# A decoder layer with GpSimd's long element-wise operations divided into pieces

## The chip, the cores and the metric

The program runs on one NeuronCore of a Trainium2 chip. Its time is the device time of one execution in microseconds (us), and a kernel's figure is the median of its runs. A core has five engines that the text names as the profile does: PE (TensorE, with PEld for its weight loads), DVE (VectorE), ACT (ScalarE), POOL (GpSimd) and SP (SyncE, which here only starts DMAs). SBUF is the on-chip memory that all engines read, PSUM the one that PE writes its products to. "Words" below are 32-bit words per partition: an operation of 128x1024 has 1024 words on each of 128 partitions.

## What is computed

One inference step of one decoder layer, for a prompt of 1024 tokens and for 8 sequences with 4 new tokens each, 1056 tokens in all with a model width of 1024. All is float32.

```python
def decoder_layer(x, cond, pos, conv_prev, s0, mla_attend, lp):
    ...
    x = x + 0.5 * mods[:, 2] * swiglu_ffn(h, lp['ffn1_wi'], lp['ffn1_wo'])
    h = rms_norm(x, lp['norm_mix']) * (1 + mods[:, 4]) + mods[:, 3]
    qkv, z, b_raw, a_raw, q_raw, ckv_raw, kr_raw = split_cols(h @ lp['w_in'], IN_SPLITS)
    gdn_out, new_conv, new_s = gdn_mixer(qkv, z, b_raw, a_raw, conv_prev, s0, ...)
    qn, qr, c, kr = mla_project(q_raw, ckv_raw, kr_raw, pos, ...)
    ctx = mla_attend(qn, qr, c, kr, lp['mla_w_uk'], lp['mla_kn_norm'])
    mla_out = jnp.einsum('bthr,rhv->bthv', ctx, lp['mla_w_uv']).reshape(B, T, MLA_HEADS * MLA_V)
    mix = jnp.concatenate([gdn_out, mla_out.astype(gdn_out.dtype)], axis=-1) @ lp['w_out']
    x = x + mods[:, 5] * mix
    ...
    x = x + 0.5 * mods[:, 8] * swiglu_ffn(h, lp['ffn2_wi'], lp['ffn2_wo'])
```

`gdn_mixer` is a gated delta rule: a short causal convolution over q, k and v, then a recurrence over a state of 64x64 words for each head, `S_t = a_t (I - b_t k_t k_t^T) S_{t-1} + b_t k_t v_t^T`, `o_t = S_t^T q_t`. The prompt's recurrence is done in chunks of 64 tokens with a triangular inverse for each chunk; the 8 short sequences take the four steps one by one. `mla_attend` is attention over latent keys, for the short sequences over 4096 cached positions that are read through a page table.

## The kernel before

The program has one stage after the other: feed-forward 1 (to about 840 us), the projections and what is done at once with their results (840 to 1290 us, `mixer_in`), the attention of the prompt (1290 to 1700 us), the recurrences (1700 to 2037 us), the output projection with feed-forward 2 behind it. Beside the prompt's attention and the recurrences, the attention of the short sequences over the cache (`sample_gen`) runs as a filler.

Each matrix product is made of three PE passes (`mm3`, L120 to L122): operands are split into a rounded high part (ACT makes `hi`, e.g. `whi`) and a remainder (`lo`, e.g. `wlo`, a subtraction on POOL or DVE).

**Projections.** `proj_weights` loads 128 columns of `w_in`, ACT casts `whi` (L645), POOL subtracts `wlo` (L646, 1024 words); three such slices are prepared ahead. PE multiplies them with the four token blocks into `pp`. What follows a slice runs as generators that are advanced between the blocks: the convolution's taps on DVE (`cy`, L885, 1080 words, three for each slice), the norms (a chain of ten small DVE operations, `rsqrt`, L697 to L701), the scaling by decay factors on POOL (`scaled`, L916, 512 words), the decay matrices (`decay`, L852), and the keys' gains (`kcat`, L1211). `mla_q_finish` takes the attention queries tile by tile, nine tiles one after the other: a DMA brings the rows `mq`, ACT squares, DVE sums and scales (L1133, L1138), POOL multiplies by the gains (L1139, 768 words), DVE and POOL rotate (`rope`: DVE L1078, L1080, L1082 and L1083, POOL L1079 and L1081), a DMA takes them away. `invert` makes the triangular inverses: POOL scales `M` (L1044), DVE runs 31 steps of two operations (`inv` L1054, `M` L1056), POOL masks the results `X` (L1060, L1064).

**Recurrences.** The prompt's recurrence `scan_gen` puts many small products on PE, with DVE operations such as `S` (L1456) between them. `gdn_sample` does the four steps of the short sequences on POOL alone: the state `gS` and its scratch `gt` have 2048 words, and each step has five operations of 2048 words and two summing trees (1024, 512, 256, 128, 64 and 32 words), all through the helper `mul` at L1515. POOL also issues the gathers of the cache (`ck`, `krh`, L628). The filler `sample_gen` needs, for each 32 keys per partition, the chain `rsqrt` on tiles `rsk` and `pv` of 128 words (DVE L699 to L701), whose end ACT copies to `rx` (L1826) for PE's `psr` (L1836).

**Order.** On POOL the operations of the three middle stages run in the order in which the program text issues them (`manual_schedule`). On the other engines and queues a planner with estimated times sets the order; each engine then works through its list in order, waiting on semaphores.

Of the kernel before, what the change touches and what calls it, by code (L numbers as in the profile page):

```python
# [12 lines left out]
ALU = mybir.AluOpType  # L13
# [4 lines left out]
P = 128  # L18
# [13 lines left out]
H = 8  # L32
# [38 lines left out]
def f(ap):  # L71
    return ap.bitcast(F32)
# [12 lines left out]
class Kernel:  # L85
# [7 lines left out]
    def pool(self, name, **kw):  # L93
        return self.ctx.enter_context(self.tc.tile_pool(reuse_waits="tile", name=name, **kw))


# [535 lines left out]
    def proj_weights(self, eng=None):  # L632

        nc = self.nc
        w = self.i["w_in"][0]
        pieces = self.worder.pop(0)
        m = sum(n for _, n in pieces)
        raw = self.wraw.tile([P, KT, P], F32, tag="wraw", name="wraw")
# [4 lines left out]
        hi = self.wsp.tile([P, KT, P], F32R, tag="w", name="whi", bufs=self.wbufs)  # L643
        lo = self.wsp.tile([P, KT, P], F32R, tag="w", name="wlo", bufs=self.wbufs)
        nc.scalar.copy(hi[:, :, :m], raw[:, :, :m])  # L645
        (eng or nc.gpsimd).tensor_tensor(out=lo[:, :, :m], in0=raw[:, :, :m], in1=f(hi[:, :, :m]), op=ALU.subtract)  # L646
        return hi, lo, m
# [181 lines left out]
    def decay(self, m, mp, tp, ps):  # L829

        nc = self.nc
# [8 lines left out]
        dm = self.r(tp, sh, "dm")  # L840
        for q in range(2):
# [3 lines left out]
            for r in range(2):  # L845
# [5 lines left out]
        yield  # L851
        nc.gpsimd.tensor_tensor(out=dm.rearrange("p t r i -> p (t r) i"), in0=dm.rearrange("p t r i -> p (t r) i"),  # L852
                                in1=self.k_lm.unsqueeze(1).to_broadcast([P, 16, 64]), op=ALU.mult)
        self.nc.sync.dma_start(out=self.dm_d[m], in_=fl)
# [57 lines left out]
    def scaled(self, tok, fac, m, t):  # L912

        t = t[:, :NP].rearrange("p (t r d) -> p t r d", r=2, d=64)
        for r in range(2):
            self.nc.gpsimd.tensor_tensor(out=t[:, :, r, :], in0=tok[:, 0:8, r, :],  # L916
                                         in1=fac[:, 0:8, 2 * m + r].unsqueeze(2).to_broadcast([P, 8, 64]), op=ALU.mult)
        return t
# [112 lines left out]
    def invert(self, tp, rp):  # L1031
# [11 lines left out]
        yield  # L1043
        nc.gpsimd.tensor_tensor(out=M, in0=M, in1=self.bi.rearrange("p (b i) -> p b i", b=2).unsqueeze(2).to_broadcast([P, 2, 32, 32]), op=ALU.mult)  # L1044
        yield
# [12 lines left out]
        for b in range(2):  # L1058
            X = self.r(rp, [P, 32, 32], "X")
            nc.gpsimd.tensor_tensor(out=X, in0=M[:, b].rearrange("p i c -> p c i"), in1=low.rearrange("p i c -> p c i"), op=ALU.mult)  # L1060
            nc.sync.dma_start(out=self.t_d[:, b], in_=X)
            yield
        X = self.r(rp, [P, 32, 32], "X")
        nc.gpsimd.tensor_tensor(out=X, in0=M[:, 0], in1=low, op=ALU.mult)  # L1064
        nc.sync.dma_start(out=self.tn_d, in_=X)
# [54 lines left out]
    def mla_q_finish(self, t, rp, tp):  # L1120
# [16 lines left out]
        for n, (d0, d1) in enumerate(((0, 64), (64, 96))):  # L1137
            nc.vector.tensor_tensor(out=q[:, 0, :, d0:d1], in0=q[:, 0, :, d0:d1], in1=ss[:, 1, n].unsqueeze(2).to_broadcast([P, H, d1 - d0]), op=ALU.mult)  # L1138
        nc.gpsimd.tensor_tensor(out=q[:, 0], in0=q[:, 0], in1=self.g_q.unsqueeze(1).to_broadcast([P, H, 96]), op=ALU.mult)  # L1139
        yield  # L1140
# [12 lines left out]
    def mla_c_post(self, row, tp, mp, ps, rp):  # L1153
# [34 lines left out]
        for t in range(NTL):  # L1188
# [21 lines left out]
            nc.vector.tensor_tensor(out=kc[:, :, 0:64], in0=pk.rearrange("p (h d) -> p h d", h=H), in1=rs.unsqueeze(2).to_broadcast([P, H, 64]), op=ALU.mult)  # L1210
            nc.gpsimd.tensor_tensor(out=kc[:, :, 0:64], in0=kc[:, :, 0:64], in1=self.g_kn.unsqueeze(1).to_broadcast([P, H, 64]), op=ALU.mult)  # L1211
            nc.gpsimd.tensor_copy(kc[:, :, 64:96], self.kr[:, t, :, :].to_broadcast([P, H, 32]))
# [280 lines left out]
    def gdn_sample(self, tp, ps, tag):  # L1493
# [20 lines left out]
        yield  # L1514
        mul = lambda out, a, b, op=ALU.mult: nc.gpsimd.tensor_tensor(out=out, in0=a, in1=b, op=op)  # L1515

# [731 lines left out]
```

## Time and profile before

| | us |
|---|---|
| median of 3 runs | 2893.67 (2882.17 to 2896.38) |
| profiled execution, its own time | 2893.45 |
| its span, first to last instruction | 2891.5 |
| PE busy | 2688.3 (93%) |
| DVE busy | 1800.7 (62%) |
| ACT busy | 1074.3 (37%) |
| POOL busy | 1027.1 (36%), 811 instructions |

An engine's busy time counts an operation from its start to its end, with whatever it waits for inside. The profile's page lists the busy time of each engine, slices of the span, the chain of waits that ended last, and groups of instructions. A group's row reads: line, engine, operation, output and inputs by the program's names, shapes, count, then busy time and the mean duration of one in ns, then the idle time of the engine before them and what ended it. The rows of a stretch show, for each engine, its busy time in that stretch with the number of its instructions in brackets, then the granted PE clock (1.00 is full), the DMA share and GB/s. A row of the view of one line shows the shortest, the median and the longest duration in ns.

### The profile page before, as it was taken

The numbers are of one execution on the slowest core, as the hardware profiler recorded it, in microseconds if no ns is written. First come the engines' busy times: TensorE is split into PE (matmuls) and PEld (weight loads), VectorE is DVE, ScalarE is ACT, GpSimd is POOL, SyncE is SP. The second block draws the span as 40 slices with busy tenths as digits, with TensorE's granted clock in tenths as the row PEclk, the third lists the DMA queues.
The fourth block names the chain that finished last, engine by engine and source line by source line (L and its number), as shares of the span: only waits on it lengthen the run. The fifth ranks groups of instructions, "written<-read, shape, count | busy, mean of one in ns | idle before, by whom it ended". The sixth has DMA issues, their size and how long they took to land.

```text
span 2891.5 us, 53252 instructions
## 1 busy us (share of the span) xinstructions
PE 2688.3 (93%) x21536; PEld 2473.8 (86%) x21536; DVE 1800.7 (62%) x3490; ACT 1074.3 (37%) x2005; POOL 1027.1 (36%) x811
## 2 busy tenths in 40 slices
PE   4999999989999897789999988888979999999999
PEld 3888989989999887788878866666979999999999
DVE  7644545455575589947766767785595555546555
ACT  5322323311144533325666654443353333331111
POOL 0222223233332444533444556550433333323331
PEclk7999999999999898899999998896889999999999
DMA  7554452333232573341212243312522222224322
GB/s 271 156 156 140 128 160 87 121 125 97 85 107 74 167 196 109 131 135 48 69 43 56 56 103 98 85 52 49 182 75 81 89 71 86 81 78 170 105 75 68
DMA packets 339488, 308.33 MB, mean 107 GB/s; under 512 B 93865, under 2 KB 282017, under 8 KB 336171
## 3 DMA queue, kind: packets, MB, share of 16 engines
q1 hardware_dynamic: 304837, 246.32, 28.1%
q10 hardware_dynamic: 28262, 37.64, 4.0%
q0 software_dynamic: 6144, 20.98, 2.3%
q8 instruction: 169, 2.77, 0.4%
q14 instruction: 76, 0.62, 0.1%
HBM read 229.29 MB, written 75.59 MB: 105 GB/s over the span
## 4 chain that ended last, share of the span: by engine, by line
PE 44%; DVE 11%; issue 3%; DMA 2%; ACT 2%; POOL 1%; ACTq 0%; SPq 0%; DVEq 0%; POOLq 0%
PE po L120 4%; PE po L121 4%; PE po L122 4%; PE pY L120 2%; PE pY L121 2%; PE pY L122 2%; PE kraw L120 2%; PE kraw L122 2%; PE kraw L121 2%; PE pX L120 1%; PE pX L121 1%; PE pZ L120 1%; PE pX L122 1%; PE pZ L122 1%; PE pZ L121 1%
## 5 line engine op out<-in xcount | busy, mean ns | idle before, releaser
L120 PE MATMUL po<-act,whi 128*128 128x264 f32 x1408 | 403.1, 286 | 9.6 <-DVE x L428 6.2
L122 PE MATMUL po<-act,wlo 128*128 128x264 f32 x1408 | 402.5, 286 | 0.0
L121 PE MATMUL po<-act,whi 128*128 128x264 f32 x1408 | 400.8, 285 | 0.0
L428 DVE SCALAR_TENSOR_TENSOR x<-po,modT,x 128x264 f32<-128x264 f32 (+1 forms) x416 | 195.6, 481 | 240.6 <-PE po L122 240.0
L120 PEld LDWEIGHTS po<-act,whi 128*128 128x128 f32 x1408 | 266.4, 189 | 10.7 <-DVE x L428 6.6
L121 PEld LDWEIGHTS po<-act,whi 128*128 128x128 f32 x1408 | 266.0, 189 | 0.0
L122 PEld LDWEIGHTS po<-act,wlo 128*128 128x128 f32 x1408 | 265.9, 189 | 0.0
L363 POOL TENSOR_TENSOR A<-wg,A 128x512 fp32r<-128x512 f32 x84 | 111.0, 1321 | 370.6 <-ACT A L362 370.6
L120 PE MATMUL pp<-hhi,whi 128*128 128x264 f32 (+1 forms) x768 | 227.3, 296 | 0.6 <-ACT ckr L681 0.6
L121 PE MATMUL pp<-hlo,whi 128*128 128x264 f32 (+1 forms) x768 | 226.7, 295 | 0.0
L122 PE MATMUL pp<-hhi,wlo 128*128 128x264 f32 (+1 forms) x768 | 224.9, 293 | 0.4 <-POOL wlo L646 0.4
L1991 DVE TENSOR_REDUCE kss<-ksq 128x8 f32<-128x512 f32 x256 | 173.3, 681 | 79.5 <-ACT ksq L1990 75.5
L104 POOL TENSOR_TENSOR wlo<-wraw,whi 128x1024 fp32r<-128x1024 f32 x39 | 97.5, 2504 | 335.9 <-ACT whi L101 263.5
L1990 ACT ACTIVATE ksq<-kraw 128x512 f32<-128x512 f32 x256 | 152.1, 598 | 169.1 <-PE kraw L122 128.4
L120 PE MATMUL pX<-B,A 128*128 128x264 f32 x704 | 203.1, 289 | 10.6 <-ACT B L362 9.7
L121 PE MATMUL pX<-B,A 128*128 128x264 f32 x704 | 202.1, 287 | 8.9 <-DVE B L363 8.9
L121 PE MATMUL pY<-T,S 128*128 128x264 f32 x704 | 200.8, 285 | 1.7 <-DVE T L363 1.7
L122 PE MATMUL pX<-B,A 128*128 128x264 f32 x704 | 200.9, 285 | 0.0
L120 PE MATMUL pY<-T,S 128*128 128x264 f32 x704 | 200.4, 285 | 0.2 <-DVE u L469 0.2
L122 PE MATMUL pY<-T,S 128*128 128x264 f32 x704 | 200.2, 284 | 0.0
L1690 POOL TENSOR_TENSOR plo<-pf,phi 128x512 fp32r<-128x512 f32 (+1 forms) x96 | 97.1, 1017 | 185.9 <-ACT phi L1689 168.1
L101 ACT CAST whi<-wraw 128x1024 fp32r<-128x1024 f32 x60 | 61.9, 1047 | 262.0 <-PE po L121 241.1
(539 smaller groups left out, 8308.4 us busy)
## 6 DMA issues: line engine op xcount, KB each, us to landing
adaw<-ada_w SPq DMA_DIRECT2D x72, 512.0 KB
wraw<-ffn_wi SPq DMA_DIRECT2D x46, 512.0 KB
act_d<-cc SPq DMA_DIRECT2D x88, 264.0 KB
wraw<-ffn_wo SPq DMA_DIRECT2D x44, 512.0 KB
wg<-ffn_wi SPq DMA_DIRECT2D x42, 512.0 KB
araw<-act_d ACTq DMA_DIRECT2D x160, 132.0 KB
x_d<-x SPq DMA_DIRECT2D x12, 1056.0 KB
wraw<-w_in SPq DMA_DIRECT2D x23, 512.0 KB
```

The lines of the kernel that those rows point to most:

```text
L101: nc.scalar.copy(hi, raw)
L104: eng.tensor_tensor(out=lo, in0=raw, in1=f(hi), op=ALU.subtract)
L120: nc.tensor.matmul(out, whi, ahi, start=first, stop=False, **kw)
L121: nc.tensor.matmul(out, whi, alo, start=False, stop=False, **kw)
L122: nc.tensor.matmul(out, wlo, ahi, start=False, stop=last, **kw)
L363: eng.tensor_tensor(out=lo, in0=src, in1=f(hi), op=ALU.subtract)
L428: nc.vector.scalar_tensor_tensor(out=x[:, d, :n], in0=ps[:, :n], scalar=self.modT[:, m, d, 0:1], in1=x[:, d, :n], op0=ALU.mult, op1=ALU.add)
L1690: nc.gpsimd.tensor_tensor(out=lo[:, off:], in0=pf[:, off:], in1=f(hi[:, off:]), op=ALU.subtract)
L1990: nc.scalar.activation(sq, kr, AF.Square)
L1991: nc.vector.tensor_reduce(out=ss[:, (j * 4 + m) * H:(j * 4 + m + 1) * H], in_=sq.rearrange("p (h d) -> p h d", h=H), axis=AX.X, op=ALU.add)
```

## The change

A new helper, `pieces`, issues one POOL operation as `n` operations on equal parts of the first free axis. Nine places use it: `wlo` in the projections (4 pieces of 256 words; where DVE does this subtraction it stays whole), `dm` in `decay` (4 of 256), `scaled` (2 of 256), `M` (8 of 256), `X` (4 of 256), `mq` (4 of 192), `kcat` (2 of 256), and in the recurrence of the short sequences every operation of over 512 words (4 of 512, or 2 of 512). What is computed is the same. The out projection's and the feed-forward's subtractions (L104, L363, L451) and the prompt attention's (L1690) are not touched.

```diff
+    def pieces(self, n, out, in0, in1, op):
+
+        w = out.shape[1]
+        for j in range(n):
+            c = slice(j * w // n, (j + 1) * w // n)
+            self.nc.gpsimd.tensor_tensor(out=out[:, c], in0=in0[:, c], in1=in1[:, c], op=op)
...
@@ proj_weights
-        (eng or nc.gpsimd).tensor_tensor(out=lo[:, :, :m], in0=raw[:, :, :m], in1=f(hi[:, :, :m]), op=ALU.subtract)
+        if eng:
+            eng.tensor_tensor(out=lo[:, :, :m], in0=raw[:, :, :m], in1=f(hi[:, :, :m]), op=ALU.subtract)
+        else:
+            self.pieces(4, lo[:, :, :m], raw[:, :, :m], f(hi[:, :, :m]), ALU.subtract)
@@ decay
-        nc.gpsimd.tensor_tensor(out=dm.rearrange("p t r i -> p (t r) i"), in0=dm.rearrange("p t r i -> p (t r) i"),
-                                in1=self.k_lm.unsqueeze(1).to_broadcast([P, 16, 64]), op=ALU.mult)
+        dv = dm.rearrange("p t r i -> p (t r) i")
+        self.pieces(4, dv, dv, self.k_lm.unsqueeze(1).to_broadcast([P, 16, 64]), ALU.mult)
@@ scaled
-            self.nc.gpsimd.tensor_tensor(out=t[:, :, r, :], in0=tok[:, 0:8, r, :],
-                                         in1=fac[:, 0:8, 2 * m + r].unsqueeze(2).to_broadcast([P, 8, 64]), op=ALU.mult)
+            self.pieces(2, t[:, :, r, :], tok[:, 0:8, r, :], fac[:, 0:8, 2 * m + r].unsqueeze(2).to_broadcast([P, 8, 64]), ALU.mult)
@@ invert
-        nc.gpsimd.tensor_tensor(out=M, in0=M, in1=self.bi.rearrange("p (b i) -> p b i", b=2).unsqueeze(2).to_broadcast([P, 2, 32, 32]), op=ALU.mult)
+        for b in range(2):
+            self.pieces(4, M[:, b], M[:, b], self.bi[:, b * 32:b * 32 + 32].unsqueeze(1).to_broadcast([P, 32, 32]), ALU.mult)
...
-            nc.gpsimd.tensor_tensor(out=X, in0=M[:, b].rearrange("p i c -> p c i"), in1=low.rearrange("p i c -> p c i"), op=ALU.mult)
+            self.pieces(4, X, M[:, b].rearrange("p i c -> p c i"), low.rearrange("p i c -> p c i"), ALU.mult)
...
-        nc.gpsimd.tensor_tensor(out=X, in0=M[:, 0], in1=low, op=ALU.mult)
+        self.pieces(4, X, M[:, 0], low, ALU.mult)
@@ mla_q_finish
-        nc.gpsimd.tensor_tensor(out=q[:, 0], in0=q[:, 0], in1=self.g_q.unsqueeze(1).to_broadcast([P, H, 96]), op=ALU.mult)
+        self.pieces(4, q[:, 0], q[:, 0], self.g_q.unsqueeze(1).to_broadcast([P, H, 96]), ALU.mult)
@@ mla_c_post
-            nc.gpsimd.tensor_tensor(out=kc[:, :, 0:64], in0=kc[:, :, 0:64], in1=self.g_kn.unsqueeze(1).to_broadcast([P, H, 64]), op=ALU.mult)
+            self.pieces(2, kc[:, :, 0:64], kc[:, :, 0:64], self.g_kn.unsqueeze(1).to_broadcast([P, H, 64]), ALU.mult)
@@ gdn_sample
-        mul = lambda out, a, b, op=ALU.mult: nc.gpsimd.tensor_tensor(out=out, in0=a, in1=b, op=op)
+        mul = lambda out, a, b, op=ALU.mult: self.pieces(max(1, int(np.prod(out.shape[1:])) // 512), out, a, b, op)
```

POOL has 816 instructions of the program before and 1037 now, 221 more: 66 from `wlo`, 12 from `dm`, 24 from `scaled`, 7 and 9 from `M` and `X`, 27 from `mq`, 8 from `kcat`, 60 and 8 from the operations of 2048 and 1024 words in the recurrence. Their order on POOL is otherwise the same. In the lists below the line numbers of the changed file are 7 to 10 higher than before, and all pieces stand at L101, the helper's line.

POOL late in the projections, where the queries' tiles, a weight slice and the inverse `X` share the queue; before:

```order
L1139 TENSOR_TENSOR mq<-mq,g_q 128x768
L878 COPY ncv<-raw 128x3
L879 COPY ncv<-raw 128x24
L646 TENSOR_TENSOR wlo<-wraw,whi 128x1024
L1079 TENSOR_TENSOR rp<-mq,k_rope 128x128
L1081 TENSOR_TENSOR rp<-mq,k_rope 128x128
L1060 TENSOR_TENSOR X<-M,low 128x1024
L1139 TENSOR_TENSOR mq<-mq,g_q 128x768
```

The same place on POOL now:

```order
L101 TENSOR_TENSOR mq<-mq,g_q 128x192 x4
L888 COPY ncv<-raw 128x3
L889 COPY ncv<-raw 128x24
L101 TENSOR_TENSOR wlo<-wraw,whi 128x256 x4
L1089 TENSOR_TENSOR rp<-mq,k_rope 128x128
L1091 TENSOR_TENSOR rp<-mq,k_rope 128x128
L101 TENSOR_TENSOR X<-M,low 128x256 x4
L101 TENSOR_TENSOR mq<-mq,g_q 128x192 x4
```

Each long operation is four in its place, and nothing else stands between the four.

POOL in the recurrence of the short sequences, at the gathers of the last steps; before:

```order
L1515 TENSOR_TENSOR gt<-gqk 128x2048
L1515 TENSOR_TENSOR gS<-gS,gt 128x2048
L1515 TENSOR_TENSOR gt<-gS,gqk 128x2048
L1515 TENSOR_TENSOR gt<-gt 128x1024
L628 DMA ck<-cache_ckv,idx 128x1024
L628 DMA krh<-cache_krope,idx 128x256
```

Now:

```order
L101 TENSOR_TENSOR gt<-gqk 128x512 x4
L101 TENSOR_TENSOR gS<-gS,gt 128x512 x4
L101 TENSOR_TENSOR gt<-gS,gqk 128x512 x4
L101 TENSOR_TENSOR gt<-gt 128x512 x2
L635 DMA ck<-cache_ckv,idx 128x1024
L635 DMA krh<-cache_krope,idx 128x256
```

The gathers stand behind as many words as before, in more operations.

The planner's order moves by a little elsewhere: 314 of PE's 19714 instructions and 137 of DVE's 3492 change places with near neighbours, most of them in the projections. One place on SP's DMA queue is the start of the output projection, where `wraw` are slices of `w_out` and `x` the residual's four blocks. Before:

```order
L110 DMA wraw<-w_out 128x8x128 x3
L168 DMA x_22590<-x_d 128x2112
L168 DMA x_22591<-x_d 128x2112
L168 DMA x_22592<-x_d 128x2112
L168 DMA x_22593<-x_d 128x2112
```

Now:

```order
L117 DMA wraw<-w_out 128x8x128
L175 DMA x_22811<-x_d 128x2112
L175 DMA x_22812<-x_d 128x2112
L175 DMA x_22813<-x_d 128x2112
L175 DMA x_22814<-x_d 128x2112
L117 DMA wraw<-w_out 128x8x128 x9
```

Two weight loads, the fifth and the sixth of this stage, now stand behind the four loads of `x`.

## The prediction

> **What bounds the kernel now.** I read the page's list of busy times first, then the granted clock and PE's idle time by stretches, then the waits of the stretch in which the largest divided operations stand, then single instructions.
>
> ```profile
> span 2891.5 us, 53252 instructions
> PE 2688.3 (93%) x21536; PEld 2473.8 (86%) x21536; DVE 1800.7 (62%) x3490; ACT 1074.3 (37%) x2005; POOL 1027.1 (36%) x811
> ```
>
> PE is the bound: 2891.5 − 2688.3 leaves 203 us in which it stood still. POOL, the only engine that the change gives more or fewer instructions, is busy 36% of the span. A change on POOL can thus move the time in two ways only: through PE's idle time, and through PE's clock. Both differ by stage. Of the stretches that follow (start:end, length, then PE, PEld, DVE, ACT, POOL busy with the number of instructions, granted clock, DMA share, GB/s), the first lies in the projections, the next two in the recurrences, the fourth in the last prompt chunks behind the short sequences' recurrence, the last in the output projection.
>
> ```profile
> 1100.00:1250.00 150.00, 116.63 (x1000) 111.17 (x998) 137.94 (x295) 53.67 (x115) 69.87 (x54) 0.84 0.41 135
> 1700.00:1850.00 150.00, 136.60 (x1486) 104.78 (x1487) 111.98 (x233) 70.38 (x143) 70.84 (x59) 0.91 0.36 99
> 1850.00:1960.00 110.00, 87.86 (x1010) 67.67 (x1010) 94.45 (x166) 47.68 (x99) 67.70 (x52) 0.89 0.24 63
> 1960.00:2000.00 40.00, 40.00 (x253) 29.91 (x252) 13.76 (x31) 9.87 (x21) 0.00 (x0) 0.52 0.30 64
> 2040.00:2050.00 10.00, 10.00 (x74) 10.00 (x73) 7.37 (x12) 6.87 (x12) 1.27 (x1) 0.86 1.01 405
> ```
>
> PE idles 33.4 us of the 150 in the projections (150 − 116.63), where DVE is busy 92%, and 13.4 + 22.1 = 35.5 us of the 260 in the recurrences. Right behind that, at 1960 to 2000, PE is never idle, but its clock is 0.52. The outer stages' long POOL operations are not touched.
>
> The waits in 1700 to 1960 (total, times, longest) name what holds PE's neighbour up there:
>
> ```profile
> POOL ck L628 <- PE psc L1873: 97.2, 3, 37.7
> ACT rx L1826 <- DVE rsk L701: 25.1, 6, 12.9
> PE psr L1836 <- ACT rx L1826: 10.6, 2, 7.7
> ```
>
> ACT waited 25.1 us for the end of the chain of `rsqrt` on DVE, and PE 10.6 us for that ACT copy. The timeline shows why the chain is slow (start, duration, engine):
>
> ```profile
> 1937.80 3.52 DVE L701 SCALAR_TENSOR_TENSOR rsk<-pv,rsk 128x128 f32<-128x128 f32 x1
> 1941.24 0.68 DVE L1970 TENSOR_TENSOR klo<-kpt,khi 128x512 fp32r<-128x512 f32 x1
> 1941.84 4.09 DVE L699 TENSOR_TENSOR pv<-rsk 128x128 f32<-128x128 f32 x1
> 1945.85 0.41 DVE L1463 TENSOR_TENSOR S<-S,pS 128x256 f32<-128x256 f32 x1
> 1946.18 3.46 DVE L700 SCALAR_TENSOR_TENSOR pv<-pv 128x128 f32<-128x128 f32 x1
> 1949.56 0.41 DVE L1456 TENSOR_TENSOR S<-S,eglK 128x256 f32<-128x256 f32 x1
> 1949.90 2.42 DVE L701 SCALAR_TENSOR_TENSOR rsk<-pv,rsk 128x128 f32<-128x128 f32 x1
> ...
> 1937.52 3.64 POOL L1515 TENSOR_TENSOR gt<-gqk 128x2048 f32<-128x2048 f32 x1
> 1941.24 4.53 POOL L1515 TENSOR_TENSOR gS<-gS,gt 128x2048 f32<-128x2048 f32 x1
> 1945.86 3.64 POOL L1515 TENSOR_TENSOR gt<-gS,gqk 128x2048 f32<-128x2048 f32 x1
> ```
>
> A DVE operation of 128 words with two inputs in SBUF that is issued while POOL runs ends about 0.15 us after POOL's operation does (1941.32 against 1941.16, 1945.93 against 1945.77): it stands still until then. At each boundary of two POOL operations, though the next starts 0.08 us later, the stuck operation ends and one or two short ones get through (`klo`, then `S`); then the next is stuck. So DVE's pace is set by the length of a POOL operation, which the change cuts to a quarter.
>
> **What a piece costs.** POOL subtracts in the prompt's attention at several widths; its widest and its narrowest group, and two of the divided groups (busy us, mean ns | idle before):
>
> ```profile
> L1690 POOL TENSOR_TENSOR plo<-pf,phi 128x512 fp32r<-128x512 f32 x48 | 61.8, 1294 | 99.0 <-ACT phi L1689 90.2 <-PE pss L122 6.1 <-PE pT L1684 1.2
> L1690 POOL TENSOR_TENSOR plo<-pf,phi 128x128 fp32r<-128x128 f32 x16 | 7.5, 467 | 22.3 <-ACT phi L1689 22.2
> L1139 POOL TENSOR_TENSOR mq<-mq,g_q 128x768 f32<-128x768 f32 x9 | 19.5, 2169 | 56.4 <-ACT zt L1218 14.2 <-DMA qk_d<-dml 14.0 <-ACT raw L866 13.8
> L1060 POOL TENSOR_TENSOR X<-M,low 128x1024 f32<-128x1024 f32 x2 | 7.7, 3857 | 9.1 <-DVE hs L699 9.1
> ```
>
> 384 words more cost 1294 − 467 = 827 ns, so a word 2.15 ns and an instruction 467 − 128 × 2.15 = 191 ns. Dividing an operation by n adds (n − 1) × 0.19 us to POOL. The 221 extra instructions make 42.2 us: 13.0 for the 68 in the recurrence, 29.2 for the 153 in the projections. POOL's busy time becomes about 1069 us. A piece of the 3.64 us operation takes (3.64 − 0.19)/4 + 0.19 = 1.05 us, one of the add of 4.53 us 1.28, of `X` 1.11, of `mq` (2.17 − 0.19)/4 + 0.19 = 0.69.
>
> **Recurrence, the unblocked chain: −17 us.** DVE's groups in 1700 to 1960, and the same operations over the whole program (shortest, median, longest ns):
>
> ```profile
> L701 DVE SCALAR_TENSOR_TENSOR rsk<-pv,rsk 128x128 f32<-128x128 f32 x19 | 22.1, 1164 | 0.3
> L700 DVE SCALAR_TENSOR_TENSOR pv<-pv 128x128 f32<-128x128 f32 x18 | 15.3, 852 | 0.3
> L699 DVE TENSOR_TENSOR pv<-rsk 128x128 f32<-128x128 f32 x18 | 12.7, 704 | 0.2
> L701 DVE SCALAR_TENSOR_TENSOR rsk<-pv,rsk x48: 273/292/3604, 1342.7 to 2014.9; 128x128 f32<-128x128 f32 x48
> ```
>
> Undisturbed such an operation takes 273 ns. Above that stand 19 × 0.891 + 18 × 0.579 + 18 × 0.431 = 16.9 + 10.4 + 7.8 = 35.1 us. How much of it stays, I replay on the timeline above: the four stuck operations took 3.52 + 4.09 + 3.46 + 2.42 = 13.5 us, 12.4 above their own 4 × 0.27. Each would now wait for the end of a piece of 1.05 to 1.28, in part used by the neighbour that got in first (0.41 to 0.68): 4 × 1.16 − (0.68 + 0.41 + 0.41) = 3.1, and 4 × 0.15 for the tails, 3.7 us, about a third. Two thirds go. What PE gains of it is bounded by two rows: by its own wait for `rx` (10.6 × 2/3 = 7) and by all its idle time there (35.5 × 2/3 = 24). I take ACT's wait, 25.1 × 2/3 = 17, between them, since what ACT is late with also delays `ksq` and with it the filler's next products. Late next is `rx`'s successor on PE, the prompt's own chain of products, which is why not all of the 24 is taken.
>
> **Clock behind it: −9 us.** At 0.52 the 40 us of 1960 to 2000 do the work of 20.8 at full clock, 19.2 lost. This stretch comes after the one in which PE idled 22.1 of 110 us. That a PE with fewer gaps ahead of it is granted more clock there is not shown by any row; the nearest are the same table's 0.91 and 0.89 where it was busy 91% and 80%. Bounds: 0 and −19; half is taken.
>
> **Recurrence, POOL's own length: +3 us.** 13.0 us more on POOL push back the gathers (`ck`, `krh`, L628) that stand behind them in its queue. The cover is POOL's wait of 97.2 us for PE ahead of the gathers; without it the 13 would all come through. Three waits are named there and the short sequences' recurrence has four steps, so I leave one step's share uncovered, 13.0/4 = 3; bounds 0 and 13.
>
> **Projections, unblocked: −8 us.** Here DVE is the neighbour to be freed:
>
> ```profile
> L885 DVE SCALAR_TENSOR_TENSOR cy<-raw,convw,cy 128x1080 f32<-128x1080 f32 x24 | 42.1, 1752 | 0.1
> L885 DVE SCALAR_TENSOR_TENSOR cy<-raw,convw,cy x36: 1215/1341/3448, 931.2 to 1242.6; 128x1080 f32<-128x1080 f32 x36
> 1118.57 3.44 DVE L885 SCALAR_TENSOR_TENSOR cy<-raw,convw,cy 128x1080 f32<-128x1080 f32 x1
> 1118.06 2.81 POOL L646 TENSOR_TENSOR wlo<-wraw,whi 128x1024 fp32r<-128x1024 f32 x1
> 1120.83 1.50 POOL L1079 TENSOR_TENSOR rp<-mq,k_rope 128x128 f32<-128x128 f32 x1
> ```
>
> The 24 taps in 1050 to 1250 stand 24 × (1.752 − 1.215) = 12.9 us above their shortest. The last three rows show that a tap pays once and POOL pays back: the tap waits 2.2 us for `wlo`, then runs its 1.2 us, and in that time POOL's `rp`, which alone takes about 0.5, stands at 1.50. Cut into four, `wlo` would let the tap in after the first piece, and the other three would wait for the tap and for what DVE has next. DVE is busy 92%, so the two take turns, and the sum of both does not shrink: I credit a fifth of the 12.9, 2.6. On the chain of waits itself (start, us) stand a norm stuck behind `X`, and two of the queries' products:
>
> ```profile
> 1211.06 3.88 DVE hs L700
> ...
> 1217.54 2.73 POOL mq L1139
> 1220.33 3.79 issue
> ...
> 1246.86 1.86 POOL mq L1139
> ...
> 1251.32 2.31 POOL wlo L646
> ```
>
> `X` runs twice; behind a piece of it `hs` waits 1.11 instead of 3.86, −5.5. Together −8; bounds 0 and −18 (all of the 12.9 and of the 5.5).
>
> **Projections, the queries' chain: +5 us.** Nine `mq` stand one after the other in a chain that ends the stage, with a weight slice behind the last (1251.32) that PE waits for. Each gets 3 × 0.19 = 0.57 us longer: 5.1. Lower bound 0 (PE still has the gate's columns to multiply), upper: at each of the three new boundaries a DVE operation of about 0.7 gets in ahead of POOL, 9 × (0.57 + 3 × 0.7) = 24.
>
> **Output projection: 0.** The planner now puts the four loads of `x` (1.08 MB each, 4.33 MB) ahead of the fifth weight slice's load; at the 405 GB/s of the stretch quoted, 10.7 us. What hides it:
>
> ```profile
> 2047.61 1.05 ACT L101 CAST whi<-wraw 128x1024 fp32r<-128x1024 f32 x1 [1.43 <-issue]
> L120 PE MATMUL po<-mhi,whi x95: 281/283/589, 2038.0 to 2074.7; 128*128 128x264 f32 x95
> ```
>
> With three passes PE does 3 × 95 products in 36.7 us, 0.129 each; a slice has 48, 6.2 us, so the fifth is due at about 2038 + 4 × 6.2 = 2063, and it was cast at 2047.6 to 2048.7. 14 us cover 10.7; with no cover it would cost that. The planner's other moves swap near neighbours on PE and DVE, 0.
>
> **Sum.** −17 − 9 + 3 − 8 + 5 = −26, so a span of 2865.5. The profiled execution's own time, 2893.45, lies 1.95 over its span and 0.2 from the median, 2893.67, so 2867 is what the median should read. Ends of all terms: −24 − 19 − 18 = −61 (2832), and −7 + 13 + 24 = +30 (2923).
>
> **The rivals.** *More is freed, 0.20:* all of PE's idle time that two thirds allow goes, the clock comes back whole and the projections give their 18, with the costs as above: −61 + 3 + 5 = −53, 2840. For it: idle time and low clock lie side by side. Against: other waits, for `ksq`, `kss` and the prompt's own products, lie in the same idle time.
>
> *Contention is only shared out, 0.18:* what DVE no longer waits, POOL does, and by POOL's 42.2 us the gathers and slices are as late as before: nothing gained, ±4, 2890 to 2898. The tap's rows at 1118 speak for it in the projections; in the recurrence POOL's 97.2 us of slack speak against.
>
> *Slower, the queries' chain, 0.09:* the place is the nine `mq`; each piece gets a DVE operation ahead of it, the 24 us above. It decides once it exceeds what the recurrence gives back, 17 + 9 − 3; with the recurrence at its low end (−7 + 3, clock 0) and the projections' −5.5 it is 24 − 9.5 = +14.5, 2908. Against: the chain of waits shows `mq` with only a few microseconds, and DVE's share of 92% leaves few operations to spare. *Pieces do not let DVE in, 0.03:* a stuck operation waits for the whole group, which is longer than the one operation was. The recurrence's 13.0 us lengthen the 70.84 + 67.70 = 138.5 us of POOL by 9%, and DVE's 35.1 us of stuck time with them, +3; with the gathers' +3 and the queries' +5 that is +11, about 2905. Against it stands that two POOL operations only 0.08 us apart already let DVE in. The Trainium skill's page "GPSIMD Engine Reference", section 2.1 "Instruction dispatch", says that an instruction's completion does not hold back the next Pool instruction, and that a core starts the next as soon as it is done with its own share; by that, pieces could run on without a gap, which is this rival. The rows at 1941 and 1945 do not agree with it as far as DVE's getting in goes.
>
> **How the numbers follow.** The forecast has 0.50, its own range 2852 to 2880 (the clock term fully or not at all, the others near their values). 0.5% is 14.5 us, about what a measurement of this kernel can tell from no change: faster means below 2879, slower above 2908. Faster: nearly all of 0.50 and 0.20, 0.70. Slower: half of the chain rival and the bad ends of the others, 0.10. The rest, 0.20, is no change. 8 in 10 lie from 2838, which cuts off the better part of the large gain, to 2893, which takes in the nearer half of the case without gain.
>
> **What would show it.** POOL at 1069 us with 1030 instructions or so; `rsk` at L701's successor in 1700 to 1960 at about 0.5 instead of 1.16 us and none longer than 1.6; ACT's wait for it below 10 us; PE's idle in the 260 us under 20; the clock behind it above 0.7; pieces of `mq` at 0.7. The prediction is wrong if DVE operations of 128 words still take 2.4 us and more in the recurrence, if the last weight slice of the projections is ready later than 1256, or if the clock behind the recurrence stays at 0.5 with PE's gaps gone.

## The result

The changed kernel takes 2863.72 us (median of 5 runs, 2860.23 to 2865.89); the kernel before, on the same chip, 2886.89 (5 runs, 2882.17 to 2896.38). The ratio is 0.9913, 95% interval 0.989 to 0.9936: faster by 0.87%, some 25 us. The forecast was 2867 us, a gain of 0.9%, and faster with a chance of 0.70.

The page of the changed kernel, its head and busy times:

```profile
span 2861.9 us, 53475 instructions
PE 2673.6 (93%) x21536; PEld 2462.5 (86%) x21536; DVE 1766.6 (62%) x3490; ACT 1074.2 (38%) x2005; POOL 1083.2 (38%) x1032
```

The span is 29.6 us shorter than the profiled one of before. POOL grew by 56 us instead of the 42 worked out, and PE, with the same instructions, shrank by 15 us: PE's busy time contains its clock. Cut at PE's own milestones (first and last product of the projections; last product of the prompt's attention to first product of the output projection), the kernel before reads (start:end, length, then PE, PEld, DVE, ACT, POOL busy, granted clock, DMA share, GB/s):

```profile
846.50:1289.00 442.50, 387.98 (x3223) 369.73 (x3221) 315.50 (x724) 172.81 (x361) 175.31 (x145) 0.90 0.45 136
1697.50:2038.00 340.50, 291.46 (x3033) 222.96 (x3031) 251.74 (x520) 142.68 (x287) 148.14 (x113) 0.84 0.29 78
```

and the changed kernel:

```profile
847.00:1285.50 438.50, 380.10 (x3231) 361.84 (x3230) 300.00 (x729) 172.97 (x361) 214.84 (x293) 0.93 0.44 134
1694.00:2008.50 314.50, 282.40 (x3029) 216.26 (x3028) 236.44 (x519) 141.56 (x285) 159.63 (x183) 0.88 0.32 86
```

The recurrences took 26 us of the gain: PE's idle time there went from 340.5 − 291.5 = 49.0 to 32.1, its busy time from 291.5 to 282.4. Busy time times clock is the same, 245 and 249 us, so the 9 us of busy time are clock. The projections took 4 us, with PE's idle time 54.5 before and 58.4 now and a clock of 0.90 before and 0.93 now. That clock cannot be put down to the change: in the kernels below whose projections are whole it lies anywhere from 0.90 to 0.93. All other stages are within 1 us of before.

DVE's chain behind `rsk`, in the changed kernel's stretch 1700 to 1960 (groups: busy, mean ns | idle), and the waits there:

```profile
L711 DVE SCALAR_TENSOR_TENSOR rsk<-pv,rsk 128x128 f32<-128x128 f32 x18 | 8.9, 497 | 0.3
L710 DVE SCALAR_TENSOR_TENSOR pv<-pv 128x128 f32<-128x128 f32 x18 | 10.0, 557 | 0.3
L709 DVE TENSOR_TENSOR pv<-rsk 128x128 f32<-128x128 f32 x18 | 7.4, 411 | 0.2
```

```profile
POOL ck L635 <- PE psc L1883: 87.6, 3, 33.0
ACT rx L1836 <- DVE rsk L711: 6.1, 5, 3.3
PE psr L1846 <- ACT rx L1836: 2.0, 1, 2.0
```

ACT's wait for the chain fell from 25.1 to 6.1 us, PE's from 10.6 to 2.0. In the same 260 us PE idled 260 − 236.7 = 23.3 us, where the forecast had 35.5 before and expected under 20:

```profile
1700.00:1850.00 150.00, 139.87 (x1556) 106.97 (x1555) 116.26 (x240) 72.34 (x147) 84.13 (x99) 0.92 0.39 106
1850.00:1960.00 110.00, 96.87 (x1071) 76.07 (x1069) 83.56 (x173) 46.02 (x96) 65.32 (x74) 0.85 0.29 71
```

But not all stuck operations are free. The timeline of the changed kernel, near the start of the recurrence (start, duration; four pieces of one operation are one row):

```profile
1749.95 3.68 DVE L1466 TENSOR_TENSOR S<-S,eglK 128x256 f32<-128x256 f32 x1 [0.52 <-PE po L1486]
1753.56 0.86 DVE L1489 TENSOR_TENSOR so<-so,po 64x256 f32<-64x256 f32 x2
...
1749.29 4.06 POOL L101 TENSOR_TENSOR gt<-gS,gqk 128x512 f32<-128x512 f32 x4
1753.50 0.99 POOL L635 DMA_INDIRECT ck<-cache_ckv,idx  x1 [0.16 <-issue]
```

`S`, 0.41 us long by itself, was issued during the first piece and ended with the fourth. Three boundaries of pieces went by without letting it in. This the forecast had ruled out, and the experiments came to turn on it.

### The profile page after: what moved, and what is told of

Read it like the earlier page. It is cut to its first block, busy times and chain, and to the rows that moved or that the text cites. A ratio compares the mean times of both kernels' runs of the same rounds, so it can differ in the third digit from the quotient of the medians.

```text
span 2861.9 us, 53475 instructions
## 1 busy us (share of the span) xinstructions
PE 2673.6 (93%) x21536; PEld 2462.5 (86%) x21536; DVE 1766.6 (62%) x3490; ACT 1074.2 (38%) x2005; POOL 1083.2 (38%) x1032
## 4 chain that ended last, share of the span: by engine, by line
PE 42%; DVE 8%; issue 5%; POOL 4%; DMA 2%; ACT 1%; SPq 0%; ACTq 0%; POOLq 0%; DVEq 0%
PE po L128 4%; PE po L129 4%; PE po L127 4%; PE pY L127 2%; PE pY L128 2%; PE pY L129 2%; PE kraw L127 2%; PE pX L127 2%; PE pX L128 2%; PE pX L129 1%; PE pZ L127 1%; PE pZ L129 1%; PE pZ L128 1%; PE kraw L129 1%; PE kraw L128 1%
## 5 line engine op out<-in xcount | busy, mean ns | idle before, releaser
L127 PE MATMUL pX<-B,A 128*128 128x264 f32 x704 | 203.9, 290 | 10.6 <-ACT B L369 9.7
```

The lines of the kernel that those rows point to most:

```text
L127: nc.tensor.matmul(out, whi, ahi, start=first, stop=False, **kw)
```

## The experiments

All ratios are to the kernel before on the same chip, with 95% intervals. "Stuck" is worked out from a trace: for all DVE operations between the last product of the prompt's attention and the first of the output projection, the time above the shortest one with the same operation, output tile and shape in that trace, summed. It is 56.7 us in the kernel before and 43.3 in the changed one. Times in microseconds come from several chips; across chips the ratios are the ones to compare.

**Which half, and how long a piece.** The change with the projections' divisions undone, with the recurrence's undone, and the first of these with other lengths of a piece (the other places of the projections are undone like `wlo`; 256 words are shown):

```diff
-            self.pieces(4, lo[:, :, :m], raw[:, :, :m], f(hi[:, :, :m]), ALU.subtract)
+            self.pieces(1, lo[:, :, :m], raw[:, :, :m], f(hi[:, :, :m]), ALU.subtract)
...
-        mul = lambda out, a, b, op=ALU.mult: self.pieces(max(1, int(np.prod(out.shape[1:])) // 512), out, a, b, op)
+        mul = lambda out, a, b, op=ALU.mult: self.pieces(max(1, int(np.prod(out.shape[1:])) // 256), out, a, b, op)
```

> Only the short sequences' recurrence is divided (pieces of 512 words, as in the change); the projections' operations are whole. Theory (DVE operations stuck behind the recurrence's long POOL operations): nearly the whole gain, 20 to 26 us under the kernel before, ACT's wait for rsk down to about 8 us. Rival 1 (the gain is the projections' doing): within 5 us of before. Rival 2 (it is the planner's other order, not the pieces): something in between, with ACT's wait for rsk not tied to it.

> Only the projections' operations are divided; the recurrence is whole. Theory: 2 to 6 us under before (the last projection product came 3.5 us earlier in the change's profile), ACT's wait for rsk still about 25 us. Rival 1 (projections): 20 us under before. Rival 2 (planner's order): anything, without a place in the profile.

> As the first, with pieces of 1024 words in the recurrence: a 2048-word operation is two, of about 1.9 us, the add's pieces 2.4. Theory: the stuck time follows the length of a piece, so about half the gain of 512 words, 10 to 14 us under before, longest rsk operation near 2.2 us. Rival (two or three more boundaries are enough, since a boundary lets two operations in): as with 512 words, 20 us or more.

> As the first, with pieces of 256 words: 104 more POOL instructions than with 512 words, 104 x 0.19 = 20 us more on POOL in the recurrence. Theory: a stuck operation waits 0.3 us or so instead of 0.5 to 0.7, worth up to 5 us more; POOL's 92 us of waiting for PE ahead of the gathers take up the 20: 22 to 30 us under before. Rival (POOL's own length is now the bound): slower than 512 words by 5 us or more, POOL's wait for psc shrinks to under 60.

| divided | median us | ratio | recurrences: length | PE idle | PE busy | clock | stuck |
|---|---|---|---|---|---|---|---|
| nothing (before) | 2890.80 | 1 | 340.4 | 49.0 | 291.3 | 0.84 | 56.7 |
| projections alone | 2886.97 | 0.9974 (0.9955 to 0.9993) | 339.1 | 49.3 | 289.8 | 0.84 | 56.8 |
| recurrence, 1024 words | 2885.68 | 0.9991 (0.9974 to 1.0007) | 327.6 | 43.9 | 283.8 | 0.86 | 50.5 |
| recurrence, 512 words | 2870.44 | 0.9934 (0.9913 to 0.9955) | 313.7 | 32.3 | 281.3 | 0.87 | 51.8 |
| recurrence, 256 words | 2852.69 | 0.9870 (0.9846 to 0.9893) | 291.5 | 26.2 | 265.3 | 0.93 | 33.6 |

The gain is the recurrence's: 512 words there alone give 0.66%, the projections alone 0.26%, beside the change's 0.87%. The rival that the gain was the projections' is out. ACT's wait for `rsk` in 1700 to 1960 was 6.3 us with 512 words in the recurrence alone; over the recurrences it was 18.9 with the projections alone, less than the 25 expected.

The length of a piece matters, but not in proportion. Halves were to give 10 to 14 us and give nothing that the time shows: the recurrences were 13 us shorter in that profile, yet the first output product came only 8 us and the end only 4 us earlier, other stages of that execution being longer. (Halves and the projections alone have 12 runs each, with medians 1.3 us apart and in the other order than their ratios, so the two cannot be told apart.) Quarters give 0.66%, eighths 1.3%.

The rival for 256 words held POOL's length to be the bound, with POOL's wait for PE ahead of the gathers under 60 us and a slower kernel. The wait did shrink, from 79.4 us with 512 words to 54.8, but the kernel was faster.

The other rival, the planner's order, is not out. Lined up one against the other, the traces have nearly all of PE's 3029 instructions of the recurrences in the order of the kernel before with 1024 words (3018 of them), 2921 with 512, 2864 with 256, and only 2553 with 128 words (below). The 1024-word kernel speaks for the pieces themselves: with the order kept, its recurrences were 13 us shorter, in one profile each, while the kernel with the projections alone, which keeps that order too, came within 1.3 us of before. For the shorter pieces no run here separates the two.

The stuck time alone does not give PE's gain either: the change and 512 words alone divide the recurrence alike and have the same idle time, 32.1 and 32.3 us, with 43.3 and 51.8 us stuck. The rows of the recurrences with 512 and with 256 words:

```profile
1700.00:2013.50 313.50, 281.33 (x3027) 216.87 (x3027) 245.94 (x518) 142.94 (x285) 157.54 (x176) 0.87 0.32 84
```

```profile
1694.00:1985.50 291.50, 265.59 (x3029) 205.19 (x3027) 227.79 (x519) 142.80 (x286) 178.23 (x284) 0.93 0.35 94
```

POOL is busy 20.7 us longer with 256 words, just the 104 × 0.19 = 20 expected, and PE has both less idle time (25.9 instead of 32.2) and more clock. Of the 22 us between the two, 16 are PE's busy time at a higher clock (busy time times clock is 245 and 247 us).

**Is it the chain on `rsk`?** Its Newton steps were left out, once with nothing divided and once with 256-word pieces (the helper hands `steps` on as the number of Newton steps):

```diff
-            self.pow_rs(rs, ss, P, 1.0 / 64, tp, bufs=1)
+            self.pow_rs(rs, ss, P, 1.0 / 64, tp, bufs=1, steps=0)
```

> The kernel before (nothing divided), with the three Newton steps left out of the rsqrt for the cached keys' norms: the nine two-input operations on rsk and pv (L699 to L701) per 32 keys are gone, 72 in all, the two one-input operations stay; part of the computation is thus left out. Theory (these are the operations that matter when they are stuck): most of the divided recurrence's gain comes without dividing anything, 20 us or more under before, and ACT's wait for rsk nearly gone. Rival (other stuck operations, S of the prompt's recurrence above all, matter as much): 5 to 12 us under before, about the 72 x 0.27 = 19 us of DVE work that partly lies on the path.

> Only the recurrence divided, in pieces of 256 words, and the same Newton steps left out. Theory (the chain on rsk is what the pieces set free): within 10 us of the undivided kernel without the steps. Rival (the pieces free S, ors and what else is stuck, and keep PE's clock up): 25 to 40 us under the undivided kernel without the steps, as much as with the steps (38).

Without dividing anything the time was 2856.63 us, 0.9895 (0.9868 to 0.9923), as the theory expected, though the work of the 72 operations themselves is gone too; but with the pieces 2830.12, 0.9806 (0.9777 to 0.9834), 26.5 us less, where the theory allowed 10. The theory falls. About half of the first gain lies outside the recurrences: the prompt's attention, beside which the same steps also run, was 18 us shorter. And the stuck time hardly moved, 54.6 us against 56.7. The operations on `ors` of the prompt's recurrence show where it went; in the kernel before, over the recurrences,

```profile
L699 DVE TENSOR_TENSOR pv<-ors 128x8 f32<-128x8 f32 x27 | 4.1, 162 | 0.3
L697 DVE TENSOR_SCALAR ors<-pv 128x8 int32<-128x8 int32 x9 | 1.5, 176 | 0.1
```

and without the steps on `rsk`

```profile
L709 DVE TENSOR_TENSOR pv<-ors 128x8 f32<-128x8 f32 x27 | 12.1, 453 | 0.3
L707 DVE TENSOR_SCALAR ors<-pv 128x8 int32<-128x8 int32 x9 | 10.2, 1142 | 0.0
```

Operations of 8 words took the place of those of 128. Whatever DVE has next while POOL is in a long operation is what waits; the row with the largest wait names the victim, not the cause.

**Shorter still, and both halves together.**

> Only the recurrence divided, in pieces of 128 words: 216 more POOL instructions than with 256, 216 x 0.19 = 41 us more on POOL in the recurrence. Theory (length of a piece sets the stuck time): with 34 us of stuck time left at 256 words, 5 to 10 us less of it. Rival (POOL itself becomes the bound): POOL waited 59.6 us for psc ahead of the gathers at 256 words, 41 more leave under 20 and some of the gathers come late: slower than 256 words by 5 us or more.

> The change with pieces of 256 instead of 512 words in the recurrence; the projections divided as in the change. If the two parts add: 38 us of the recurrence and 4 to 7 of the projections, 42 to 45 under before, a ratio of 0.985. If the projections' part was only chance in the order: 38, as without it.

128 words: 2868.11 us, 0.9933 (0.9909 to 0.9957), by the ratios some 18 us slower than 256. Neither expectation had the reason. POOL's wait for PE ahead of the gathers was still 52.0 us, not under 20 as the rival had it. POOL's last piece of the recurrence, though, ended at 1959.3 us, 26 us later than with 256 words; what that costs here is not settled. And the stuck time rose from 33.6 to 50.0 us. Two single operations make nearly 22 us of it. The larger, in the timeline of this kernel:

```profile
1874.83 12.27 DVE L717 TENSOR_SCALAR pv<-kss 128x128 f32<-128x128 f32 x1
1887.13 0.69 DVE L1979 TENSOR_TENSOR klo<-kpt,khi 128x512 fp32r<-128x512 f32 x1
...
1873.73 2.96 POOL L101 TENSOR_TENSOR gS<-gS,gt 128x128 f32<-128x128 f32 x7
1876.63 5.79 POOL L101 TENSOR_TENSOR gt<-gS,gqk 128x128 f32<-128x128 f32 x16
1882.36 5.88 POOL L101 TENSOR_TENSOR gt<-gt 128x128 f32<-128x128 f32 x14
```

An operation of 0.23 us was stuck for 12.27, through some thirty pieces. The three groups overlap: 1873.73 + 2.96 ends at 1876.69, and the next group began at 1876.63. In the kernel before, an operation that needs the last one's result started 0.08 us after it (1941.16 to 1941.24 in the forecast's rows). That is the difference that suggests itself: pieces of one operation do not depend on each other, and a piece of 128 words of the next operation depends on one that ended long ago, so POOL does not wait, and by the records starts each piece about 0.04 us before the last has ended. Counting, in the traces of before and of the six kernels with all steps whose recurrence is divided in the change's order, the boundaries at which a DVE operation was clearly stuck: where POOL's next operation came after a gap, the DVE operation got in at 112 of 112; where it overlapped, at 194 of 222 with pieces of 256 to 1024 words, and at 52 of 121 with 128. What is called clearly stuck moves the counts at the overlaps by a tenth and more, and hardly the gaps. Nor are the boundaries independent: with 128 words the two longest waits alone passed by 55 of them. The Trainium skill's "GPSIMD Engine Reference", section 2.1 "Instruction dispatch", which says that completion of an instruction does not hold back the next Pool instruction, agrees with the overlapping rows.

With 256 words and the projections' divisions the time was 2852.15 us, 0.9883 (0.9861 to 0.9906): the two do not add there.

**Gaps put back.** If the missing gaps are the cause, putting the dependent operations next to each other must help the short pieces. The recurrence was written piece by piece, so that POOL waits for its own result at one of two boundaries, or two of three; the summing trees stayed as they were (256 words are shown):

```diff
+        def chunks(steps, count):
+            done = 0
+            for j in range(8):
+                c = slice(j * 64 // 8, (j + 1) * 64 // 8)
+                for out, a, b, op in steps:
+                    nc.gpsimd.tensor_tensor(out=out[:, c], in0=a[:, c], in1=b[:, c], op=op)
+                while done < count * (j + 1) // 8:
+                    done += 1
+                    yield
...
-            mul(S, S, al[:, t:t + 1].unsqueeze(2).to_broadcast([P, 64, 32]))
-            yield
-            mul(t1, S, kb)
-            yield
...
+            yield from chunks([(S, S, alb, ALU.mult), (t1, S, kb, ALU.mult)], 2)
...
+            yield from chunks([(t1, kb, vb, ALU.mult), (S, S, t1, ALU.add), (t1, S, qb, ALU.mult)], 3)
```

> Only the recurrence divided, pieces of 128 words as in the run before this with 128, but taken piece by piece through the dependent operations: gS times decay, then gt, for one piece after the other, and gt, gS, gt likewise, so that at 1 of 2 or 2 of 3 boundaries POOL waits for its own last result. Theory formed from the 128-word run (a stuck DVE operation gets in for certain only where POOL's next instruction waits; in a stream of independent pieces, each starting before the last has ended, it can stay out to the stream's end): no DVE operation stuck for over 4 us (the summing trees are still streams), 10 to 18 us faster than the 128-word run, about 2850 to 2858. Rival (POOL's length was the loss at 128 words): the waits add some 165 x 0.6 x 0.12 = 12 us to POOL, so slower than 2868.

> The same order with pieces of 256 words. Theory: few operations were stuck over a boundary at 256 words, so within 6 us of 2853 either way. Rival (POOL's length): 5 to 10 us slower than 2853.

> The same order with pieces of 512 words. Theory: the operations stuck through a whole group of four (S 4.0 us, pv 4.0 us in the 512-word run) are gone, worth up to 8 us: 2860 to 2870. Rival (a boundary of any kind lets in, the long ones were chance): 2870.

| pieces | in the change's order | stuck | piece by piece | stuck |
|---|---|---|---|---|
| 128 words | 2868.11, 0.9933 | 50.0 | 2863.54, 0.9913 (0.9883 to 0.9942) | 30.0 |
| 256 words | 2852.69, 0.9870 | 33.6 | 2845.11, 0.9853 (0.9822 to 0.9884) | 29.6 |
| 512 words | 2870.44, 0.9934 | 51.8 | 2874.41, 0.9939 (0.9919 to 0.9960) | 47.6 |

On the stuck time the theory holds: at 128 words it falls by 20 us, the longest `S` from 9.96 to 0.75 us, and in all three kernels the DVE operation got in at every one of the 98 boundaries with a gap. On the time it does not show: by the ratios 6 us at 128 words, where 10 to 18 were expected, and 5 at 256, with intervals that overlap, and nothing at 512. The recurrences' rows with 128 words, first in the change's order, then piece by piece:

```profile
1693.50:2007.50 314.00, 276.31 (x3028) 209.53 (x3027) 243.41 (x518) 142.62 (x286) 210.37 (x498) 0.90 0.33 87
```

```profile
1689.50:2003.00 313.50, 286.96 (x3050) 218.78 (x3050) 228.29 (x528) 142.68 (x288) 217.88 (x506) 0.88 0.32 85
```

PE's idle time fell from 37.7 to 26.5 us, as much as at 256 words, but PE's busy time rose by as much, at a lower clock. Why the clock was lower with fewer gaps is not settled by these runs, and PE's order differs more here than anywhere (2315 of the 3029 instructions as before). But one thing had become long: POOL. From the chain of waits that ended last, piece by piece with 128 words (start, us), and the row of the stretch behind it:

```profile
1963.92 0.83 POOL gt L1542 x2
...
1965.75 5.00 POOL gt L101 x12
...
1970.93 4.06 SPq L1563
1975.09 4.02 SPq L1564
...
1981.18 2.48 DMA gqk<-smpo_d
1983.68 0.64 ACT osq L1359
```

```profile
1975.00:2003.00 28.00, 13.98 (x119) 9.85 (x117) 19.89 (x70) 7.13 (x13) 2.34 (x1) 0.57 0.25 47
```

From 1932 to 1971 that chain runs through POOL with no wait of over 0.3 us, then through the short sequences' result on its way out to memory and back. POOL's last piece ended at 1972.8 us, 13.5 us later than in the change's order, about the 12 us that the rival of that expectation had worked out, and 39 us later than with 256 words. So the rival, POOL's length, is right in part: piece by piece with 128 words, POOL has no cover left behind its last gather.

**The fastest.** The last two ideas together:

> The recurrence in pieces of 256 words taken piece by piece through the dependent operations, and the projections divided as in the change. If the projections' part adds to the recurrence's (0.9853 and 0.9974): 0.983, some 50 us under before and faster than the change by 0.8%. If it does not add, as with 256-word pieces in the change's order (0.987 without and 0.9883 with it): 0.985 to 0.987.

It takes 2848.80 us, 0.9846 (0.9820 to 0.9872). It is faster than the change (the intervals do not touch), and the same within its interval as 256 words piece by piece without the projections.

## Why the forecast was right, and where it was not

*The stuck operations, −17.* PE's idle time in the whole stage of the recurrences fell by 49.0 − 32.1 = 16.9 us, but in the 260 us for which the term was worked out by 35.5 − 23.3 = 12.2. The way there was less right than the number. Two thirds of the time stuck in the `rsk` chain were to go; by the groups above, 35.1 us above 273 ns became 18 × (0.497 + 0.557 + 0.411 − 3 × 0.273) = 11.6, which is two thirds; but over all operations the stuck time fell only from 56.7 to 43.3, because others (`ors`, `S`) took turns in being stuck. The step that failed is the replay's premise that each boundary lets DVE in. The rows at 1941 and 1945 on which it rested are of operations that need the last one's result; the pieces of one operation do not. The rival that denied it got 0.03; its mechanism is real for some boundaries at 512 words and for most at 128, and the short streams, four pieces here, kept it cheap: the longest, `S`, lost 3.3 us.

*The clock, −9.* PE's busy time in the recurrences fell by 9.1 us at the same work. The term was half of a bound, chosen without a row for it; that it met to a tenth is luck. The stretch that the forecast spoke of shows the change, before:

```profile
1935.00:1945.00 10.00, 6.59 (x67) 4.83 (x67) 9.90 (x9) 0.98 (x3) 9.45 (x8) 1.00 0.00 0
1945.00:1955.00 10.00, 2.20 (x21) 1.37 (x21) 9.45 (x10) 2.62 (x5) 9.53 (x7) 0.61 0.00 0
1955.00:1965.00 10.00, 9.78 (x78) 7.85 (x77) 7.09 (x23) 2.81 (x7) 0.51 (x2) 0.50 0.70 114
1965.00:1975.00 10.00, 10.00 (x61) 8.00 (x61) 4.33 (x12) 0.96 (x2) 0.00 (x0) 0.50 0.38 84
1975.00:1985.00 10.00, 10.00 (x52) 7.36 (x52) 1.87 (x4) 1.56 (x3) 0.00 (x0) 0.50 0.14 40
1985.00:1995.00 10.00, 10.00 (x66) 6.83 (x64) 3.33 (x5) 3.50 (x8) 0.00 (x0) 0.50 0.05 15
1995.00:2005.00 10.00, 10.00 (x85) 7.18 (x84) 4.43 (x8) 5.40 (x11) 0.00 (x0) 0.83 0.19 54
```

and after:

```profile
1935.00:1945.00 10.00, 8.13 (x101) 6.17 (x99) 9.97 (x21) 4.34 (x9) 9.92 (x10) 1.00 0.60 101
1945.00:1955.00 10.00, 7.61 (x79) 5.92 (x79) 6.99 (x18) 1.69 (x4) 2.62 (x5) 0.66 0.46 97
1955.00:1965.00 10.00, 10.00 (x51) 6.95 (x51) 2.21 (x4) 1.19 (x2) 0.00 (x0) 0.79 0.20 54
```

Before, the last burst of POOL left PE 2.20 us of work in ten, the clock fell, and it stayed at 0.50 for 40 us in which PE was idle for 0.2 us. After, the end of the burst left PE 8.13 and 7.61 us of work, and the clock was back at 0.79 in the next ten. In these two kernels the longer gap and the longer stretch at half clock stand together. That the gap brings the clock down is not shown, and the last kernel of the experiments, 256 words piece by piece with the projections, speaks against it. There the clock fell as far at the same place, with PE idle for 0.8 us in the twenty around the fall:

```profile
1915.00:1925.00 10.00, 9.73 (x109) 7.38 (x107) 9.54 (x26) 5.34 (x11) 9.08 (x16) 1.00 0.11 28
1925.00:1935.00 10.00, 9.48 (x86) 7.71 (x86) 5.93 (x15) 1.70 (x4) 9.45 (x14) 0.59 0.12 18
1935.00:1945.00 10.00, 10.00 (x38) 7.39 (x38) 1.77 (x3) 0.60 (x1) 4.07 (x8) 0.50 0.64 96
1945.00:1955.00 10.00, 10.00 (x56) 6.25 (x55) 3.40 (x5) 3.88 (x9) 0.00 (x0) 0.54 0.40 111
```

Nor do the whole recurrences' idle time and clock go together: that kernel has 21.9 us and 0.88, 256 words in the change's order 26.2 us and 0.93. What sets the clock here stays open, though at 256 words it is the larger part of what was gained over 512. The Trainium skill's "TensorE: Matmul & The Clock Gate", Part 1, has the gate fall after an idle window of about 3.4 us and rise after one busy window. These traces bear out neither. A mean clock of 0.61 in 1945 to 1955 is 2.2 us at 1.00 and the rest at 0.50, so the fall came at about 1947.2, when PE's longest gap, the 6.49 us ahead of the product at 1953.65, had only begun. In the last kernel there was no such gap. And 40 us at 0.50, busy by the profile, did not bring the clock up.

```profile
1953.65 0.38 PE L1917 MATMUL pjm<-ident,mst 128*7 128x128 f32 x1 [6.49 <-ACT ksq L1990]
```

*POOL's length, +3 and the size of a piece.* A 512-word piece in the recurrence took what was worked out; in the projections pieces were longer (groups of the changed kernel):

```profile
L101 POOL TENSOR_TENSOR gt<-gS,gqk 128x512 f32<-128x512 f32 x32 | 32.8, 1055 | 0.2
L101 POOL TENSOR_TENSOR mq<-mq,g_q 128x192 f32<-128x192 f32 x36 | 28.5, 820 | 42.2 <-issue 22.8 <-ACT raw L897 13.5 <-ACT tok L913 5.9
L101 POOL TENSOR_TENSOR wlo<-wraw,whi 128x256 fp32r<-128x256 f32 x88 | 78.9, 926 | 38.7 <-ACT whi L652 38.5
```

1.055 us against 1.05, but `mq` 0.82 against 0.69, and `wlo` 0.93 against (2.57 − 0.19)/4 + 0.19 = 0.79. The short ones of `mq`, 23 of the 36, take 0.59 to 0.60 us; of the 13 longer ones, up to 1.64, all but one run beside DVE operations that read two tensors, which fits POOL waiting for DVE. `mq` makes 4 us and `wlo` 10, about the 14 by which POOL's busy time missed (1083 against 1069). This is what the rival of a contention that is only shared out had said of the projections. The recurrence's 11 us more on POOL are not seen on PE's path; the wait of 87.6 us for PE is still there.

*The projections, −8 and +5.* The sum, −3, met the −4 of the stage, but no run shows its terms. PE's idle time there rose by 3.9 us and its busy time fell by 7.9. But PE's busy time in the stage is 380 to 388 us in the kernels with whole operations as well. In all profiled kernels together the stage is 439.4 to 442.4 us long with whole operations (10 kernels) and 434.5 to 438.1 with pieces (4), 5 us apart in the mean, with idle times of 54 to 62 and 54 to 58. In the mean PE has 2.4 us less idle and 2.7 us less busy time with pieces; what the single terms are is not settled.

*The output projection, 0.* The stage of 104.2 us before took 104.0.

So the sum met the result within a few microseconds, 2867 against 2863.7, with the place right (the recurrences), one premise wrong and two terms, the clock's and the projections', met without a mechanism that the runs show.

## What to carry to other kernels

Where GpSimd's long operations hold up VectorE, dividing them can pay even though each piece costs 0.19 us, as long as GpSimd has slack; the best length is found by trying, and here it was half of the change's. VectorE gets in where GpSimd stops between pieces: an operation that needs the last piece's result, put behind it, freed VectorE at every such place here, though the time did not show it beyond its interval. Long streams of independent short pieces kept VectorE out the longest. Read TensorE's idle time and its clock apart, since here they did not always move together, and look at what else moved: a planner that reorders other engines is part of what is measured. And do not take the operation with the longest wait for the cause: with its work taken out, the next one waited in its place.

## What the runs showed of the hardware beyond the forecast

A VectorE operation with a single tensor input was held up as well: the `TENSOR_SCALAR` on `pv` above, 12.27 us instead of 0.23. The reductions `kss` were not: 256 of them lie between 0.656 and 0.690 us in that same kernel.

```profile
L717 DVE TENSOR_SCALAR pv<-kss x16: 216/229/12267, 1339.4 to 1981.2; 128x128 f32<-128x128 f32 x16
L2000 DVE TENSOR_REDUCE kss<-ksq x256: 656/685/690, 1316.4 to 1980.0; 128x8 f32<-128x512 f32 x128
```

By the records of these traces independent GpSimd operations in a row overlap by about 0.04 us, dependent ones leave about 0.08 us between them, and a waiting VectorE operation got in at each gap counted but only at a part of the overlaps. What decides at an overlap stays open.
